# A down projection over a sliding range of input block pairs

## The chip, the cores and the metric

The kernel runs on one core of a Trainium2 chip. The metric is the device time of one execution in microseconds (us), the median of several runs. TensorE multiplies, VectorE (DVE), ScalarE (ACT) and GpSimd (POOL) work elementwise, and SyncE (SP) and ScalarE issue the DMAs that move data between HBM and the on-chip memory.

## The reference

The input is x, 1024 tokens by 1024 features in float32. Two layers follow, the first with a chunked bidirectional mLSTM as its mixer, the second with windowed attention, each followed by a dense feed-forward block; every block begins with an RMS norm and is added to x. The change touches the feed-forward blocks:

```python
D_FF = -(-(8 * D_MODEL) // (3 * 256)) * 256   # 2816

def swiglu(h, w_in, w_out):
    gu = h @ w_in
    gate, up = gu[..., :D_FF], gu[..., D_FF:]
    return (jax.nn.silu(gate) * up) @ w_out

for i in range(DEPTH):                        # DEPTH = 2
    hn = rmsnorm(x, norm_mix_w[i])
    x = x + ...                               # mLSTM (i = 0) or windowed attention (i = 1)
    x = x + swiglu(rmsnorm(x, norm_ffn_w[i]), ffn_w_in[i], ffn_w_out[i])
return rmsnorm(x, norm_final_w)
```

## The kernel before

**Arithmetic.** A float32 product is made of three passes over operands that are split into a high and a low part: high by high, high by low, low by high. Splitting takes ScalarE for the high part (a copy into the rounded type, L203) and VectorE for the low part (the difference, L204). All matmuls are 128x128 weights by 512 columns.

**Feed-forward block.** The 2816 hidden features are 22 blocks of 128, taken as 11 pairs (p, p + 11). The down projection (`ffn_down`, L683) makes its eight output row blocks in pairs (e, e + 4), e = 0..3. For each it runs a 2x2 Strassen-Winograd step (`strassen`, L567 on): seven products in place of eight, summed over the input pairs. One pair costs 7 products by 3 passes = 21 matmuls. The products come in the order a11 b11, s4 b22, a12 b21, s2 t2, s1 t1, s3 t3, a22 t4, where a and s are blocks and sums of the weights, b and t blocks and sums of the hidden rows.

**Chunks and steps.** The 11 pairs are three chunks, `CHUNKS = ((0, 4), (4, 8), (8, 11))`; for each chunk e runs over 0..3, so FFN 0 has 12 steps: eight over four pairs, four over three. In FFN 1 the last chunk goes through `down_plain` (L742, matmuls on L759) in token halves, with no Strassen step. Each step reads two row blocks of x from memory (`xkeep`, L711), adds its products (L714 to L726) and writes them back (L730).

**Forms.** The hidden rows b and t are kept in HBM (`hkeep`), four tiles for each pair: the up projection writes them. `hidden_forms` (L545) loads those of the next chunk (hraw) during the last step of a chunk and splits them: for each pair one split of 512 columns (f) and three of 1024 (fh, fl). They then serve four steps. `left` (L507) makes the weight forms of the next step: wah/wal (needed by the first product), wch/wcl (s3, s4), wbh/wbl (s1, s2) and wd, from sums s12 and s34. Forms, weights, x and raw loads are units of a shared pool (46 units of 128 x 1032 floats); the four pairs of a chunk hold 28.

**Norm behind FFN 0.** In the last four steps each finished row block is scaled and split for the next product (`norm_split_row`: hnh on L207, hnl on L208) and its square is added to R (`norm_square_row`: L299 on ScalarE, L300 on VectorE). `norm_sums` (L372) then sums R over partitions by TensorE, and `spread` (L384 to L391) turns the result into a row factor. The attention's first product (L231) follows; its weights are cut into wh (L190, ScalarE) and wl (L191, GpSimd).

**Order.** Each engine takes its instructions in a fixed order. The program is written as above with small callbacks between the products (`more` for a part of the next weights, `rolled` for a group of forms, `taken` for adds to x); the tile framework sets the order on each engine when the program is built, from the order in which it is written, the dependencies of tiles, and when a pool has a free unit. An instruction that waits holds all behind it on its engine.

Of the kernel before, what the change touches and what calls it, by code (L numbers as in the profile page):

```python
# [11 lines left out]
F32 = mybir.dt.float32  # L12
# [24 lines left out]
CHUNKS = ((0, 4), (4, 8), (8, 11))  # L37
# [7 lines left out]
def _pieces(n, bits):  # L45
    rest = Fraction("6.28318530717958647692528676655900576839433879875021164194988918461563281257")
    out = []
    for _ in range(n):
        step = Fraction(2) ** (math.floor(math.log2(float(rest))) - bits + 1)
        q = (rest / step).__floor__() * step  # L50
        out.append(float(q))
        rest -= q
    return out

# [28 lines left out]
class Trunk:  # L83
# [32 lines left out]

    def slab(self, dtype=F32, name="slab"):
        return Pair([self.unit(dtype, name) for _ in range(2)])
# [24 lines left out]
    def sources(self):  # L143
        h = self.h
        cols = lambda src: [src[:, o:o + D] for o in range(0, src.shape[-1], D)]
        out = [h["m_gate"]]
        for u in range(3 * NH):
            out += cols(h["m_in"][u])
        for u in range(4):
            out += cols(h["m_out"][u])  # L150
        ffn = [[], []]
        for i in range(2):
            for p in range(NP):
                for f in (p, p + NP):
                    ffn[i] += cols(h["ffn_in"][i, f])
            for p0, p1 in CHUNKS:
                ffn[i] += [h["ffn_out"][i, d, :, 2 * p0 * P:2 * p1 * P] for d in D_ORDER]
# [170 lines left out]
    def norm_forms(self, i):  # L328
# [10 lines left out]
        f12 = pair("f12")  # L339
        ya = self.unit(name="ya")  # L340
        A.activation(ya, xa, AF.Copy, scale=wa)
        t12, t34 = self.unit(name="t12"), self.unit(name="t34")
# [153 lines left out]
    def left(self, m=HALF):  # L496
# [3 lines left out]
        a11, a12, a21, a22 = g[:, lo_], g[:, hi_], u[:, lo_], u[:, hi_]  # L500
        wide = (lambda: self.t([P, S], F32, "s", self.spare)) if self.spare else (lambda: self.unit(name="s"))
        s12, s34 = wide(), wide()
        pair = lambda n: tuple(self.unit(F32R, n + x)[:, :2 * m] for x in "hl")
        two = lambda f, c: (f[0][:, c], f[1][:, c])
        out = {}

        def one():  # L507
            wa = pair("wa")
            self.split(*wa, g)
            out["a11"], out["a12"] = two(wa, lo_), two(wa, hi_)  # L510
            V.tensor_tensor(s12[:, lo_], a21, a22, op=ALU.add)
            V.tensor_tensor(s12[:, hi_], s12[:, lo_], a11, op=ALU.subtract)

        def two_():
            V.tensor_tensor(s34[:, lo_], a11, a21, op=ALU.subtract)
            V.tensor_tensor(s34[:, hi_], a12, s12[:, hi_], op=ALU.subtract)
            wc = pair("wc")
            self.split(*wc, s34[:, :2 * m])
            out["s3"], out["s4"] = two(wc, lo_), two(wc, hi_)

        def three_():
            wb = pair("wb")
            self.split(*wb, s12[:, :2 * m])
            out["s1"], out["s2"] = two(wb, lo_), two(wb, hi_)

        def four():
            wd = self.unit(F32R, "wd")
            out["a22"] = (wd[:, :m], wd[:, m:2 * m])
            self.split(*out["a22"], a22)
# [15 lines left out]
    def hidden_forms(self, i, p0, p1):  # L545
        lo_, hi_ = slice(0, HALF), slice(HALF, S)
        forms = [{} for _ in range(p0, p1)]
# [6 lines left out]
        def single(p):  # L554
            raw = load(p, 0, lo_)
            f = self.unit(F32R, "f1")
            forms[p - p0]["b11"] = f[:, lo_], f[:, hi_]
            self.split(f[:, lo_], f[:, hi_], raw)

        def double(p, j, a, b):  # L560
# [3 lines left out]
            forms[p - p0][a] = f[0][:, lo_], f[1][:, lo_]  # L564
            forms[p - p0][b] = f[0][:, hi_], f[1][:, hi_]

        def group(f, *args):  # L567
            return lambda: [f(p, *args) for p in range(p0, p1)]

        return forms, [group(single), group(double, 1, "b21", "b22"), group(double, 2, "t1", "t2"), group(double, 3, "t3", "t4")]  # L570


    def hidden_plain(self, i, p0, p1):
# [8 lines left out]
        todo = [(p, j) for j in range(2) for p in range(p0, p1)]  # L582
# [42 lines left out]
    def ffn_up(self, i, side=()):  # L625
# [5 lines left out]
        plain = CHUNKS[-1][0] if i else NP  # L631
        forms = self.forms
        for n in range(NF):
            p, second = n // 2, n % 2
            roll = ()
            if n + 1 < NF:
                nxt, todo = self.left()
            else:
                nxt, todo = self.left((CHUNKS[0][1] - CHUNKS[0][0]) * P)
                self.dforms, roll = self.hidden_forms(i, *CHUNKS[0])  # L640
            more = lambda: todo.pop(0)() if todo else None
            hs = self.unit(name="hs")
# [28 lines left out]
            elif p < plain:  # L671
                t12, t34 = self.unit(name="t12"), self.unit(name="t34")
# [3 lines left out]
                V.tensor_tensor(t34[:, lo_], hs[:, hi_], ha[:, hi_], op=ALU.subtract)  # L676
                V.tensor_tensor(t34[:, hi_], hs[:, lo_], t12[:, hi_], op=ALU.subtract)
                nc.scalar.dma_start(self.hkeep[i][p][3], t34)
# [5 lines left out]
    def ffn_down(self, i, which, final=False):  # L684
# [3 lines left out]
        cur, forms = self.cur, self.dforms  # L688
        for ci, (p0, p1) in enumerate(CHUNKS):
            last = ci == len(CHUNKS) - 1  # L690
            if last:
                self.norm_begin(which, "final" if final else "plain")
                if final:
                    self.down_plain(p0, p1)
                    return
                self.x = [None] * KT
            for e in range(4):
                nxt, todo, roll = None, [], ()
                if e < 3:
                    nxt, todo = self.left((p1 - p0) * P)  # L700
                elif not last:
                    q0, q1 = CHUNKS[ci + 1]
                    if final and ci + 2 == len(CHUNKS):
                        roll = self.hidden_plain(i, q0, q1)
                    else:
                        nxt, todo = self.left((q1 - q0) * P)
                        nforms, roll = self.hidden_forms(i, q0, q1)
                more = lambda: todo.pop(0)() if todo else None
                xa, xb = self.unit(name="x"), self.unit(name="x")
                for x, d in ((xa, e), (xb, e + 4)):  # L710
                    nc.sync.dma_start(x, self.xkeep[d])  # L711

                def one(st):
                    V.tensor_tensor(xa[:, lo_], xa[:, lo_], st["a"], op=ALU.add)  # L714
                    V.tensor_tensor(xa[:, hi_], xa[:, hi_], st["c"], op=ALU.add)
                    V.tensor_tensor(xa[:, hi_], xa[:, hi_], st["e"], op=ALU.add)  # L716
                    G.tensor_tensor(xa[:, hi_], xa[:, hi_], st["u2"], op=ALU.add)  # L717

                def two(st):
                    V.tensor_tensor(xb[:, hi_], xb[:, hi_], st["c"], op=ALU.add)  # L720
                    G.tensor_tensor(xb[:, hi_], xb[:, hi_], st["u3"], op=ALU.add)

                def three_(st):
                    u3 = st["u3"]
                    V.tensor_tensor(u3, st["d"], u3, op=ALU.add)
                    V.tensor_tensor(xb[:, lo_], xb[:, lo_], u3, op=ALU.add)  # L726

                self.strassen(cur, forms, more, roll, (one, two, three_))
                for x, d in ((xa, e), (xb, e + 4)):
                    nc.scalar.dma_start(self.xkeep[d], x)  # L730
                    if last:
                        self.x[d] = x
                        self.norm_split_row(d)
                        self.norm_square_row(d)
                cur = nxt
            if not last:
                forms = nforms if nxt else None
        self.norm_end()

    def down_plain(self, p0, p1):  # L740
        nc = self.nc
        hs = [self.hs[p, j] for j in range(2) for p in range(p0, p1)]  # L742
# [468 lines left out]
    def rope_tables(self):  # L1211
# [3 lines left out]
        ang, kh, r1, kl = (self.t([P, Q], F32, f"tab{i}", 1) for i in range(4))  # L1215
# [307 lines left out]
    def run(self):  # L1523
        self.setup()
        self.mlstm()
        with self.phase("f0", 9, dict(mm=6, mx=2), 2):
            self.attn_setup()
            self.ffn_up(0, self.rope_tables())
# [27 lines left out]
def arrange(inp):  # L1556
# [19 lines left out]
    for hh in range(NH):  # L1576
# [21 lines left out]
    order = [f + o for p0, p1 in CHUNKS for o in (0, NP) for f in range(p0, p1)]  # L1598
    out["ffn_out"] = np.ascontiguousarray(
        fo.reshape(2, NF, P, KT, P)[:, order].transpose(0, 3, 2, 1, 4)  # L1600
    ).reshape(2, KT, P, NF * P)
# [20 lines left out]
```

## Time and profile before

| | |
|---|---|
| median of 3 runs | 2376.28 us (2373.6 to 2376.89) |
| profiled execution, its own time | 2373.66 us |
| its span | 2371.7 us |
| TensorE busy | 2199.7 us, 93% |
| weight loads busy (beside the matmuls) | 1789.9 us, 75% |
| VectorE busy | 1645.4 us, 69% |
| ScalarE busy | 902.7 us, 38% |
| GpSimd busy | 554.1 us, 23% |
| mean granted TensorE clock | 0.967 |

The span is the stretch from the first to the last instruction that the profile shows; about 2 us of the execution lie around it. FFN 0's down projection runs from 964 to 1206 us, FFN 1's from 2099 to the end. Times in rows are counted from the span's start.

### The profile page before, as it was taken

The page shows a single profiled execution, that of the slowest core. Times are in us where ns is not written, and L with a number is a line of the kernel's source. Part 1 is how long each engine was busy: PE and PEld are TensorE (multiplying, and loading weights), DVE is VectorE, ACT ScalarE, POOL GpSimd, SP SyncE. Part 2 cuts the span into 40 slices and gives each one's busy share as a digit, 9 for nine tenths or more (in the row PEclk, how much of TensorE's full clock was granted, in tenths as well). Part 3 has the DMA queues.
Part 4 walks back from the last instruction along what each step waited for, and adds up shares of the span by engine and source line. Part 5 has one row for each costly group of instructions (what it writes and reads, how often), then busy time and mean ns, then how long its engine had stood idle before and what let it go on. Part 6 is the DMA issues. An engine that isn't in the chain of part 4 may idle for free. (4 is left out here: it accounts for less than half of the span.)

```text
span 2371.7 us, 28532 instructions
## 1 busy us (share of the span) xinstructions
PE 2199.7 (93%) x10379; PEld 1789.9 (75%) x10379; DVE 1645.4 (69%) x2954; ACT 902.7 (38%) x1616; POOL 554.1 (23%) x398
## 2 busy tenths in 40 slices
PE   6999998989999999899979888799899999999988
PEld 3889888867888888677758666587788888867767
DVE  5455666698777777777863666787877777677723
ACT  3334445343222222432422666774422222242322
POOL 4312213301111111111123444560111111111133
PEclk9999999999999999999979899999999999999999
DMA  3111114133232323675624233702223232266552
GB/s 118 51 36 45 63 36 151 50 108 107 95 120 98 116 98 132 231 260 180 226 102 146 67 114 104 239 17 98 89 98 126 88 133 98 82 212 247 182 191 72
DMA packets 95788, 286.12 MB, mean 121 GB/s; under 512 B 10736, under 2 KB 17776, under 8 KB 95648
## 3 DMA queue, kind: packets, MB, share of 16 engines
q1 hardware_dynamic: 73960, 209.71, 27.0%
q10 hardware_dynamic: 21688, 74.59, 7.9%
q8 instruction: 82, 1.34, 0.2%
q14 instruction: 58, 0.48, 0.1%
HBM read 191.53 MB, written 92.73 MB: 120 GB/s over the span
## 5 line engine op out<-in xcount | busy, mean ns | idle before, releaser
L191 POOL TENSOR_TENSOR wl<-raw,wh 128x1024 fp32r<-128x1024 f32 (+2 forms) x56 | 128.6, 2301 | 352.9 <-ACT wh L190 283.5
L651 POOL TENSOR_TENSOR t<-t,R 128x512 f32<-128x512 f32 x44 | 63.9, 1452 | 613.3 <-ACT t L650 613.3
L231 PE MATMUL mm<-slab,wh 128*128 128x512 f32 x512 | 153.5, 409 | 11.1 <-ACT wh L190 8.3
L539 PE MATMUL mm<-f,wah 128*128 128x512 f32 x504 | 159.3, 397 | 3.2 <-DVE x L793 2.4
L539 PE MATMUL mm<-f12h,wbh 128*128 128x512 f32 x352 | 138.8, 395 | 0.4 <-ACT wbh L203 0.4
L539 PE MATMUL mm<-f12l,wbh 128*128 128x512 f32 x352 | 138.8, 394 | 0.0
L539 PE MATMUL mm<-f12h,wbl 128*128 128x512 f32 x352 | 138.5, 394 | 0.0
L607 DVE TENSOR_TENSOR t<-mm,t 128x512 f32<-128x512 f32 x64 | 44.2, 691 | 128.0 <-PE mm L539 128.0
L231 PE MATMUL mm<-hnh,wh 128*128 128x512 f32 x416 | 127.8, 409 | 1.6 <-ACT wh L190 1.6
L650 ACT ACTIVATE t<-t 128x512 f32<-128x512 f32 x44 | 27.9, 634 | 256.3 <-DVE t L649 256.3
L231 PE MATMUL mm<-hnl,wh 128*128 128x512 f32 x416 | 125.2, 402 | 0.0
L231 PE MATMUL mm<-hnh,wl 128*128 128x512 f32 x416 | 124.6, 399 | 0.0
L231 PEld LDWEIGHTS mm<-slab,wh 128*128 128x128 f32 x512 | 96.3, 194 | 33.6 <-ACT wh L190 10.1
L596 ACT ACTIVATE t<-mm 128x512 f32<-128x512 f32 x64 | 38.4, 600 | 215.2 <-PE mm L539 197.6
L539 PE MATMUL mm<-f34h,wd 128*128 128x512 f32 x352 | 117.2, 394 | 0.0
L1404 POOL TENSOR_TENSOR e<-e,smd 128x768 f32<-128x768 f32 (+1 forms) x64 | 87.4, 1368 | 123.2 <-DVE smd L1403 78.2
L539 PEld LDWEIGHTS mm<-f,wah 128*128 128x128 f32 x504 | 95.1, 189 | 26.4 <-ACT wah L203 4.5
L1392 DVE CUSTOM_DVE_ANT_0 e<-sc,mask,nsink 128x384 f32<-128x384 f32 (+1 forms) x128 | 72.8, 577 | 46.2 <-PE sc L1387 44.9
L539 PE MATMUL mm<-f,wal 128*128 128x512 f32 x252 | 100.7, 400 | 4.2 <-DVE wal L204 4.2
L717 POOL TENSOR_TENSOR x<-x,t 128x512 f32<-128x512 f32 x20 | 30.2, 1512 | 308.4 <-DVE x L716 163.4
L1387 PE MATMUL sc<-slab,slab 128*128 128x384 f32 (+1 forms) x256 | 68.1, 348 | 33.9 <-DMA slab<-bounce 21.2
L203 ACT ACTIVATE wah<-raw 128x1024 fp32r<-128x1024 f32 (+1 forms) x64 | 66.5, 1039 | 74.5 <-DMA hkeep<-hs 33.2
(330 smaller groups left out, 6381.8 us busy)
## 6 DMA issues: line engine op xcount, KB each, us to landing
raw<-in_ffn_in_dram SPq DMA_DIRECT2D x88, 512.0 KB
hraw<-hkeep SPq DMA_DIRECT2D x63, 512.0 KB
xkeep<-x ACTq DMA_DIRECT2D x56, 512.0 KB
hkeep<-hs ACTq DMA_DIRECT2D x44, 512.0 KB
x<-xkeep SPq DMA_DIRECT2D x40, 512.0 KB
hkeep<-t ACTq DMA_DIRECT2D x38, 512.0 KB
raw<-in_ffn_out_dram SPq DMA_DIRECT2D x32, 512.0 KB
raw<-in_m_in_dram SPq DMA_DIRECT2D x24, 512.0 KB
```

The source lines that it names most:

```text
L191: (nc.vector if fast else nc.gpsimd).tensor_tensor(lo[:, c], r[:, c], hi[:, c].bitcast(F32), op=ALU.subtract)
L203: self.nc.scalar.activation(hi, src, AF.Copy)
L231: self.nc.tensor.matmul(st["ps"], lhsT=l, rhs=r, start=j == 0, stop=j == len(jobs) - 1)
L539: self.nc.tensor.matmul(ps, lhsT=l[a][:, c], rhs=r[b], start=start and k + a + b == 0, stop=stop and k == last and a == 1, skip_group_chec ...
L596: A.activation(p1, pa, AF.Copy)
L607: V.tensor_tensor(u2, pb, p1, op=ALU.add)
L650: A.activation(g0, g0, AF.Silu)
L651: G.tensor_tensor(g0, g0, R0, op=ALU.mult)
L717: G.tensor_tensor(xa[:, hi_], xa[:, hi_], st["u2"], op=ALU.add)
L1387: T.matmul(ps[:, :n], lhsT=lq, rhs=kk[:, j * S + k0 * P:j * S + (k0 + nk) * P], start=j == 0, stop=j == 1,)
L1392: V.tensor_tensor_reduce(out=e[:, hd, :n], in0=ps[:, :n], in1=self.mask[:, m0:m0 + n], scale=1.0, scalar=self.nsink[:, s], op0=ALU.add, op ...
L1404: G.tensor_tensor(e[:, j:j + 2, :n], e[:, j:j + 2, :n], d.unsqueeze(2).broadcast_to([P, 2, n]), op=ALU.mult,)
```

## The change

The chunks go. A table gives for each step its output pair and its input pairs; the range of pairs slides, and a step loads and splits only the pairs that the step before did not hold. FFN 0 still has 12 steps (the first over three pairs, eight over four, three over three), FFN 1 eight steps over four pairs and then the same plain tail. Pair 0 is loaded and split a second time in FFN 0, pairs 0 and 1 in FFN 1. The matmul count stays 10297; SyncE issues 537 DMAs in place of 525. The down weights lie in HBM in the order of the steps.

```diff
-CHUNKS = ((0, 4), (4, 8), (8, 11))
+STEPS = (
+    ((0, (0, 1, 2)), (1, (0, 1, 2, 3)), (2, (0, 1, 2, 3)), (3, (1, 2, 3, 4)),
...
+    ((0, (0, 1, 2, 3)), (1, (0, 1, 2, 3)), (2, (1, 2, 3, 4)), (3, (2, 3, 4, 5)),
...
+)
+PLAIN = (8, 9, 10)
...
-    def norm_square_row(self, d):
+    def norm_square_row(self, d, eng=None):
...
-            nc.vector.tensor_tensor(self.R, self.R, sq, op=ALU.add)
+            (eng or nc.vector).tensor_tensor(self.R, self.R, sq, op=ALU.add)
...
         def one():
-            wa = pair("wa")
+            s12, s34 = st["s"] = wide(), wide()
+            V.tensor_tensor(s12[:, lo_], a21, a22, op=ALU.add)
+            V.tensor_tensor(s12[:, hi_], s12[:, lo_], a11, op=ALU.subtract)
+            V.tensor_tensor(s34[:, lo_], a11, a21, op=ALU.subtract)
+            V.tensor_tensor(s34[:, hi_], a12, s12[:, hi_], op=ALU.subtract)
+            wa = unit("wah"), unit("wal")
             self.split(*wa, g)
...
-            elif p < plain:
-                t12, t34 = self.unit(name="t12"), self.unit(name="t34")
+            elif not i or p not in PLAIN:
+                t12 = self.wide("t12")
...
+                V.tensor_tensor(ha[:, hi_], hs[:, hi_], ha[:, hi_], op=ALU.subtract)
+                V.tensor_tensor(ha[:, lo_], hs[:, lo_], t12[:, hi_], op=ALU.subtract)
+                nc.scalar.dma_start(self.hkeep[i][p][3], ha)
...
+        steps = STEPS[i]
+        for n, (e, pairs) in enumerate(steps):
+            last = n + 4 >= len(steps) and not final
+            end = n + 1 == len(steps)
...
+            if not end:
+                after = steps[n + 1][1]
+                nxt, todo = self.left(len(after) * P)
+                new, roll = self.hidden_forms(i, [p for p in after if p not in pairs])
+            elif final:
+                new, roll = {}, self.hidden_plain(i, PLAIN)
...
+            E = V if end else G
+
+            def keep(x, d):
+                nc.scalar.dma_start(self.xkeep[d], x)
+                if last:
+                    self.x[d] = x
+                    self.norm_split_row(d)
+                    self.norm_square_row(d, E)
...
+                E.tensor_tensor(xa[:, hi_], xa[:, hi_], st["u2"], op=ALU.add)
+                keep(xa, e)
...
+                E.tensor_tensor(xb[:, hi_], xb[:, hi_], st["u3"], op=ALU.add)
...
                 V.tensor_tensor(u3, st["d"], u3, op=ALU.add)
                 V.tensor_tensor(xb[:, lo_], xb[:, lo_], u3, op=ALU.add)
+                if end and not final:
+                    self.ahead()
+                keep(xb, e + 4)
...
+            live = {p: f for p, f in live.items() if not end and p in after}
+            live.update(new if not end else {})
...
-        with self.phase("f0", 9, dict(mm=6, mx=2), 2):
+        with self.phase("f0", 9, dict(mm=6, mx=2), 3):
```

`ahead` cuts the next weight (wh, wl) before it is asked for. Of the square sums five go to GpSimd (the first of the eight is a copy, the last step's two stay on VectorE). The last argument of `phase` is the number of spare wide tiles for s, two before, three now; the rotary tables' four small tiles become one unit. Lines behind `strassen` shift by 18 to 21: L539 becomes L557, L204 L222, L372 L390, L231 L249; the adds to x are L735 to L738 (u2), L742, L743 (u3), L747 and L748.

The order on VectorE as FFN 0 enters its ninth step, before (a chunk seam; x_9518 and x_9519 are the row blocks of the eighth step, wal is the ninth's):

```order
L204 TENSOR_TENSOR wal_9566<-raw_9378,wah_9565 128x768
L714 TENSOR_TENSOR x_9518<-x_9518,mm_9522 128x512
L607 TENSOR_TENSOR t_1698_9614<-mm_9601,t_1678_9535 128x512
L204 TENSOR_TENSOR fl_9586<-hraw_9583,fh_9585 128x1024
L715 TENSOR_TENSOR x_9518<-x_9518,mm_9616 128x512
L720 TENSOR_TENSOR x_9519<-x_9519,mm_9616 128x512
L716 TENSOR_TENSOR x_9518<-x_9518,mm_9552 128x512
L616 TENSOR_TENSOR t_1711_9669<-mm_9601,t_1678_9535 128x512
L204 TENSOR_TENSOR fl_9592<-hraw_9589,fh_9591 128x1024
L725 TENSOR_TENSOR t_1711_9669<-mm_9677,t_1711_9669 128x512
L726 TENSOR_TENSOR x_9519<-x_9519,t_1711_9669 128x512
```

The weights' low part wal is made ahead of the eighth step's adds to x. Now, at the same place (x_9505 is the second row block of the eighth step, wal the ninth's weights, f and fl its new pairs):

```order
L742 TENSOR_TENSOR x_9505<-x_9505,mm_9595 128x512
L222 TENSOR_TENSOR f_1675_9525<-hraw_9523,f_1675_9525 128x512
L747 TENSOR_TENSOR t_1700_9641<-mm_9649,t_1700_9641 128x512
L748 TENSOR_TENSOR x_9505<-x_9505,t_1700_9641 128x512
L222 TENSOR_TENSOR f_1677_9530<-hraw_9528,f_1677_9530 128x512
L222 TENSOR_TENSOR wal_9553<-raw_9343,wah_9552 128x1024
L222 TENSOR_TENSOR fl_9571<-hraw_9568,fh_9570 128x1024
L222 TENSOR_TENSOR fl_9577<-hraw_9574,fh_9576 128x1024
L222 TENSOR_TENSOR fl_9611<-hraw_9608,fh_9610 128x1024
L222 TENSOR_TENSOR fl_9617<-hraw_9614,fh_9616 128x1024
L222 TENSOR_TENSOR wcl_9626<-s_9547,wch_9625 128x1024
```

What moved is wal: it stands behind L747 and L748, the last adds of the eighth step, which take that step's last product, and behind a split of the new pairs.

TensorE at the end of FFN 0, before (L539 is the last down product, L372 the sums of the norm, L389 and L390 the spread, L231 the attention's first product):

```order
L539 MATMUL mm_10170<-fl_9705,wd_10077 128x512
L539 MATMUL mm_10170<-fh_9704,wd_10077 128x512
L372 MATMUL mx_10253<-ones,R_9715 128x1 x4
L372 MATMUL mx_10268<-ones,R_9715 128x1 x4
L389 MATMUL mx_10318<-t_1839_10308,ones 128x512
L390 MATMUL mx_10318<-t_1840_10309,ones 128x512
L389 MATMUL mx_10332<-t_1842_10322,ones 128x512
L390 MATMUL mx_10332<-t_1843_10323,ones 128x512
L231 MATMUL mm_10222<-hnh_9829,wh_10218 128x512
L231 MATMUL mm_10222<-hnh_9954,wh_10218 128x512
```

Now, from the last down product on (L249 is the attention's first product):

```order
L557 MATMUL mm_10187<-fl_10089,wd_10102 128x512
L557 MATMUL mm_10187<-fh_10088,wd_10102 128x512
L249 MATMUL mm_10231<-hnh_9773,wh_10201 128x512
L249 MATMUL mm_10231<-hnh_9904,wh_10201 128x512
L249 MATMUL mm_10231<-hnh_10048,wh_10201 128x512
```

Nineteen rows further on, all of L249 (L390 are the sums of the norm, L249 into mm_10292 the second half):

```order
L249 MATMUL mm_10231<-hnh_10206,wh_10201 128x512
L249 MATMUL mm_10231<-hnl_10207,wh_10201 128x512
L249 MATMUL mm_10231<-hnh_10206,wl_10202 128x512
L390 MATMUL mx_10262<-ones,R_9680 128x1 x4
L249 MATMUL mm_10292<-hnh_9773,wh_10201 128x512
L249 MATMUL mm_10292<-hnh_9904,wh_10201 128x512
L390 MATMUL mx_10277<-ones,R_9680 128x1 x4
L249 MATMUL mm_10292<-hnh_10048,wh_10201 128x512
L249 MATMUL mm_10292<-hnh_10167,wh_10201 128x512
```

The product's first 24 matmuls moved ahead of the norm's sums, and the second half begins between them.

## Rows read from the trace of the kernel before

**Rows 1.** The page, part 1: busy time of each engine.

```profile
PE 2199.7 (93%) x10379; PEld 1789.9 (75%) x10379; DVE 1645.4 (69%) x2954; ACT 902.7 (38%) x1616; POOL 554.1 (23%) x398
```

**Rows 2.** Stretches: us, busy us and count of each engine, clock, DMA, GB/s.

```profile
964.45:995.33 30.88, 23.98 (x85) 16.93 (x83) 24.75 (x30) 15.07 (x18) 0.83 (x1) 0.89 0.54 173
995.33:1016.84 21.51, 20.15 (x84) 15.73 (x85) 20.30 (x26) 7.13 (x9) 6.22 (x4) 1.00 0.74 263
1036.28:1055.76 19.48, 19.48 (x86) 15.77 (x84) 10.02 (x14) 5.70 (x8) 3.27 (x2) 1.00 0.89 306
1055.76:1083.58 27.82, 23.45 (x85) 17.02 (x84) 22.16 (x24) 15.88 (x18) 0.05 (x1) 0.88 0.58 209
1142.00:1161.73 19.73, 17.26 (x64) 12.74 (x63) 15.70 (x19) 10.43 (x13) 0.40 (x1) 0.91 0.57 207
1161.73:1176.49 14.76, 14.76 (x65) 11.75 (x63) 14.76 (x21) 7.32 (x9) 3.26 (x2) 1.00 0.38 145
...
2098.83:2128.11 29.28, 23.76 (x85) 16.96 (x84) 22.51 (x26) 16.93 (x19) 0.83 (x1) 0.88 0.52 175
2186.96:2215.67 28.71, 23.81 (x85) 17.42 (x84) 20.81 (x23) 15.78 (x18) 0.06 (x1) 0.88 0.57 201
2278.72:2294.82 16.10, 11.53 (x39) 8.18 (x39) 1.85 (x3) 3.23 (x4) 5.71 (x4) 0.82 0.98 352
```

**Rows 3.** Timeline of TensorE at the seam of 1055.76: start, us, operation, wait.

```profile
1059.41 0.50 PE L539 MATMUL mm<-fh,wah 128*128 128x512 f32 x1 [0.69 <-ACT t L596]
...
1066.04 0.79 PE L539 MATMUL mm<-fh,wch 128*128 128x512 f32 x1 [2.55 <-ACT wch L203]
...
1068.43 0.79 PE L539 MATMUL mm<-fh,wcl 128*128 128x512 f32 x1 [0.65 <-DVE wcl L204]
...
1070.73 0.63 PE L539 MATMUL mm<-fl,wch 128*128 128x512 f32 x1
1071.16 0.63 PE L539 MATMUL mm<-fh,wcl 128*128 128x512 f32 x1
```

**Rows 4.** Stretches behind two seams, columns as in rows 2.

```profile
1065.54:1072.37 6.83, 5.68 (x12) 3.92 (x13) 6.80 (x9) 6.65 (x8) 0.00 (x0) 0.50 0.78 300
1150.87:1154.29 3.42, 3.42 (x10) 2.64 (x9) 3.35 (x6) 3.42 (x6) 0.00 (x0) 0.50 0.45 183
```

**Rows 5.** Stretch and timeline at the end of FFN 0, all engines.

```profile
1206.44:1242.33 35.89, 18.72 (x69) 14.88 (x69) 15.94 (x44) 7.29 (x8) 11.73 (x8) 0.67 0.19 66
...
1210.62 0.69 DVE L725 TENSOR_TENSOR t<-mm,t 128x512 f32<-128x512 f32 x1 [2.15 <-POOL x L721]
...
1217.29 1.84 PE L372 MATMUL mx<-ones,R 128*128 128x1 f32 x8 [10.85 <-DVE R L300]
...
1224.99 0.76 PE L389 MATMUL mx<-t,ones 128*128 128x512 f32 x1 [3.74 <-issue]
...
1229.72 3.29 PE L231 MATMUL mm<-hnh,wh 128*128 128x512 f32 x7 [1.63 <-ACT wh L190]
...
1242.33 0.86 PE L231 MATMUL mm<-hnh,wh 128*128 128x512 f32 x3
```

**Rows 6.** Costs by form: VectorE and GpSimd; rows of the square sums; ScalarE's cuts.

```profile
L204 DVE TENSOR_TENSOR fl<-hraw,fh 128x1024 fp32r<-128x1024 f32 x33 | 38.7, 1219 | 5.2 <-ACT fh L203 5.2
L204 DVE TENSOR_TENSOR wbl<-s,wbh 128x1024 fp32r<-128x1024 f32 x8 | 12.0, 1504 | 1.0 <-DMA xkeep<-x 1.0
...
L204 DVE TENSOR_TENSOR f<-hraw,f 128x512 fp32r<-128x512 f32 x7 | 4.7, 689 | 4.6 <-ACT f L203 4.6
...
L191 POOL TENSOR_TENSOR wl<-raw,wh 128x1024 fp32r<-128x1024 f32 x47 | 113.5, 2415 | 338.7 <-ACT wh L190 283.5 <-PE pk L215 38.0 <-issue 15.8
...
L300 DVE TENSOR_TENSOR R<-R,sq x21: 1211/1219/3435, 495.0 to 1674.4; 128x1024 f32<-128x1024 f32 x21
...
1209.77 1.15 ACT L207 ACTIVATE hnh<-x,nw 128x1024 fp32r<-128x1024 f32 x1 [6.91 <-POOL x L717]
...
1228.62 2.00 ACT L190 ACTIVATE wh<-raw 128x1024 fp32r<-128x1024 f32 x2
```

More of the change, by code (lines that the diff above doesn't have):

```diff
@@ L53, in _pieces, with down_order @@
     return out
+def down_order(i):
+    out = [(d, pairs) for e, pairs in STEPS[i] for d in (e, e + 4)]
+    return out + [(d, PLAIN) for d in D_ORDER] if i else out
 def weave(main, fill=()):
@@ L115, in unit, with wide @@
         return self.sl.tile([P, UNIT], dtype, name=self.nm(name), tag="unit")[:, :S]
+    def wide(self, tag):
+        return self.unit(name=tag)
     def slab(self, dtype=F32, name="slab"):
@@ L155, in sources @@
                     ffn[i] += cols(h["ffn_in"][i, f])
[L156 to L157 removed]
+            at = 0
+            for d, pairs in down_order(i):
+                ffn[i].append(h["ffn_out"][i, :, at:at + 2 * len(pairs) * P])
+                at += 2 * len(pairs) * P
         att = []
@@ L542, in seven, with hidden_forms @@
                 )
-    def hidden_forms(self, i, p0, p1):
+    def hidden_forms(self, i, pairs):
         lo_, hi_ = slice(0, HALF), slice(HALF, S)
-        forms = [{} for _ in range(p0, p1)]
+        forms = {p: {} for p in pairs}
         def load(p, j, cols):
@@ L580, in get @@
             self.split(*self.hs[p, j], raw)
-        todo = [(p, j) for j in range(2) for p in range(p0, p1)]
+        todo = [(p, j) for j in range(2) for p in pairs]
         n = -(-len(todo) // 4)
@@ L638, in ffn_up @@
             else:
-                nxt, todo = self.left((CHUNKS[0][1] - CHUNKS[0][0]) * P)
-                self.dforms, roll = self.hidden_forms(i, *CHUNKS[0])
+                pairs = STEPS[i][0][1]
+                nxt, todo = self.left(len(pairs) * P)
+                self.dforms, roll = self.hidden_forms(i, pairs)
             more = lambda: todo.pop(0)() if todo else None
-            hs = self.unit(name="hs")
+            hs = self.wide("hs")
             R0, R1 = self.Rv(0), self.Rv(1)
@@ L687, in ffn_down @@
         lo_, hi_ = slice(0, HALF), slice(HALF, S)
[L688 to L695, printed above, removed]
-                self.x = [None] * KT
[L697 to L737, printed above, removed]
@@ L741, in down_plain @@
+        if final:
+            self.norm_begin(which, "final")
+            self.down_plain(PLAIN)
+        else:
+            self.norm_end()
+    def down_plain(self, pairs):
         nc = self.nc
-        hs = [self.hs[p, j] for j in range(2) for p in range(p0, p1)]
+        hs = [self.hs[p, j] for j in range(2) for p in pairs]
         self.load_x(self.xkeep)
@@ L1214, in rope_tables @@
         Q = S // 4
-        ang, kh, r1, kl = (self.t([P, Q], F32, f"tab{i}", 1) for i in range(4))
+        tab = self.unit(name="tab")
+        ang, kh, r1, kl = (tab[:, i * Q:(i + 1) * Q] for i in range(4))
         def put(i, tab):
@@ L1597, in arrange @@
     ).reshape(2, NF, P, 2 * D)
[L1598 to L1601, printed above, removed]
+    fo = fo.reshape(2, NF, P, KT, P)
+    out["ffn_out"] = np.stack([
+        np.concatenate([fo[i, p + o, :, d] for d, pairs in down_order(i) for o in (0, NP) for p in pairs], axis=1)
+        for i in range(2)
+    ])
     return out
```

66 lines of the change are left out of this document (38 added, 28 removed), and 3 rows, old and new, of the table STEPS.

## Prediction

> **What bounds the kernel now.** I read the page's shares first, then the table of stretches cut at the starts of the down projection's steps, then TensorE's timeline at the seams, then the costs by form. TensorE is busy 93% of the span [rows 1]: nothing gets faster here unless TensorE waits less, for the change keeps its matmul count. A step over four input pairs is 84 matmuls. Undisturbed it takes 19.48 us, over three pairs 14.76 us [rows 2], which is 0.232 us a matmul and 4.87 us a pair. The steps that begin a chunk are longer: 30.88 us behind the up projection and 27.82 and 19.73 us at the two chunk seams of FFN 0, 29.28 and 28.71 us in FFN 1 [rows 2]. Over the undisturbed step these lose 11.4, 8.3, 5.0, 9.8 and 9.2 us; with 2.0 us in the second step (21.51) FFN 0 loses 26.7 us and FFN 1 19 us and a little.
>
> What a seam loses is seen in rows 3. TensorE waits 0.69 us for ScalarE's copy of the first product, 2.55 us for the high part of the next weights (wch, queued behind six fh splits) and 0.65 us for wcl (behind the fl splits on VectorE). Then its clock falls: from 1070.73 to 1071.16 one matmul takes 0.43 us instead of 0.23. The stretches at granted clock 0.50, the 1.2 GHz level, are 6.83 us behind waits of about 4 us and 3.42 us behind waits of 2.5 us [rows 4]; a matmul there costs 0.2 us more, so 3.2 and 1.6 us. The second step, 2.0 us late, kept clock 1.00 [rows 2]: short waits need not bring the clock down.
>
> The other loss is the end of FFN 0. From the last down matmul (1206.44) to the third half of the attention's first product (1242.33) pass 35.89 us, for 48 product matmuls and 12 of the norm. TensorE waits for the last square sums until 1217.29, for the spread of the row factor until 1224.99, and for the first cut weight until 1229.72; clock 0.67 [rows 5].
>
> **The change part by part.** All sums start at the profiled execution, 2373.66 us (2.6 below the median, inside the runs' 2373.6 to 2376.89).
>
> End of FFN 0. The 24 matmuls of the first half now stand ahead of the norm's sums, 22 of the second ahead of the spread. They need the cut weight: with u2 and u3 added on VectorE the two GpSimd adds, on which L725 waited 2.15 us [rows 5], leave the path, and the cut is issued in the last step. From rows 6, two trailing adds 1.4, hnh 1.15, two cuts (2.00 us together) and their handovers: the first product about 4.8 us behind the last down matmul. Then 48 matmuls at 0.232 (11.1), sums 3.7 (two groups at the times of rows 5), spread 0.8: 20.4; about half of it at the low clock, +3: 23.4 against 35.9. I take -12.5. Ends: -6 (all 48 at 0.43) and -15.5 (none).
>
> First step. Now over three pairs: 63 matmuls, 14.6 us, while VectorE's 24.75 us of work there [rows 2] stays: one pair's splits (0.69 and three of 1.22, 4.35 us, rows 6) go to the next step, which begins a pair's matmuls earlier. Ends: 0, when the same VectorE work takes the same time, and +4.9, a pair's matmuls no longer beside it. I take +3.5.
>
> Sliding steps. I call them s0 to s11. The intent is that VectorE's bursts are spread: a seam's 22.16 us of VectorE [rows 2] becomes 10 to 15 us a step plus 4.35 per new pair, under 19.5 everywhere. But the order on VectorE changes too. At the seam before, wal of the next step stands ahead of x's adds; now, where new pairs come in, it stands behind L747 and L748, and L747 waits for the step's very last product. So the third matmul of the next step waits for two adds, f and wal, three times 0.69 (the 512-column form) and 1.22 [rows 6], less the 0.46 us of two matmuls: 2.8 us. Behind it follow the old seam's waits, with two pairs' splits instead of four: 0.7 for the copy, then wch and wcl, 2.7 by adding durations along the queues. With an allowance of 0.5 us for GpSimd's u3 and the low clock (1.5, the shorter stretch of rows 4) this is about 8 us for s4 and s8 each, where before lost 8.3 and 5.0. The same order with one new pair stands ahead of s5 and s11 (wal 3.5 us late by the queue, clock +1.5 to +2: 5.5 and 5); s3 and s7 wait 1.3 each for the copy and wch; s9 and s10, over three pairs, where VectorE is busy all of 14.76 us already [rows 2], 1.9 each. Sum: 16+10.5+2.6+3.8=33 against 13.3 (8.3 and 5.0): +19.7. Ends: -8 (only 0.7 for the copy at seven steps) and +27 (every wait over 2 us brings the 6.83 us stretch).
>
> The sums of squares go to GpSimd in three of the last four steps: five adds. VectorE loses four of 1.22, GpSimd gains five of about 2.4 (its 1024-wide form, rows 6). VectorE's R add itself has a longest case of 3.435 against 1.219 [rows 6], and wbl a mean of 1.504: such operations run long where GpSimd adds at the same time. The Trainium skill ("SBUF — State Buffer", "Who interferes with whom") says that a VectorE instruction with two SBUF inputs and a GpSimd instruction that reads SBUF exclude each other, the later one waiting out the first. By that rule the move gives nothing back, five times 2.4 us of lockout for four of 1.22; the trace agrees as far as the 3.435 us case goes. In the sum: 0, ends -2 and +5, since the last three steps have 1.2 us adds on either side.
>
> FFN 1. The range slides at five places. The seam at 2186.96 (9.2) gives way to about 13.7 (0.6, 3.5, 6, 0.6, 2.5 and some clock, by the same queue sums): +4.5, ends -6 and +9. Its plain tail, 16.10 us at clock 0.82 with DMA 0.98 busy [rows 2], has the first cut weight behind five splits of the hidden rows: +1.5, ends 0 and +3. Up projections (t34 in place, one more spare): an allowance of +0.4, ends -1 and +2. Twelve loads of 512 KB come twice, 6 MB: DMA share in the steps is 0.5 to 0.9, no term.
>
> Sum: -12.5+3.5+19.7+0+4.5+1.5+0.4=+17.1, 2391 us.
>
> **The rivals.** First, the spreading does what it is for: waits for wal hide, since GpSimd and ScalarE are ahead in a step that is not a burst. Sliding steps then lose the 0.7 us copy and little else: FFN 0 -8, FFN 1 -6, end -12.5, first step +3.5, tail +1.5: -21.5, 2352; with half of the wal waits left (five of 2.8, half: 7, and the clock twice: 3) 2362. For it: VectorE's sum per step fits, 10.02 us in a step without splits [rows 2]. Against: wal's place in the queue is fixed, however fast the engines are.
>
> Second, the waits come but the clock stays, as in the second step before (2.0 us, clock 1.00): the slides lose 6.3 us less, FFN 1 2, the first step 3.2 and the end 3: 17.1-14.5=+2.6, 2376, no change to be seen.
>
> Third, slower than forecast: the units run out. 46 units carry 28 live forms, eight of weights, x and raw; with a sliding range new forms are taken while old ones are still read. If the load of the new pairs waits for a unit that the last product frees, each of eleven sliding steps gets a load's wait; the seam shows 2.55 us for a queue of splits [rows 3], so 11 x 2.5=27 in place of some 10 that the forecast already holds: 2408. It decides where the hidden rows' loads start only when TensorE enters the next step. "Perfetto Trace Analysis" of the Trainium skill ("Optimization Strategy") reads a gap that repeats regularly on the engine that should be full as too little SBUF for the next tile. Before there are no such gaps inside a chunk (19.48 us steps), so nothing shows it yet.
>
> **How the numbers follow.** Forecast (slower by 6 to 30 us) 0.56; first rival 0.24; second 0.10; third 0.10. A difference under 0.2%, 4.8 us, can't be told from none here: faster 0.24, within 0.10, slower 0.66. Range 2360 to 2408: below it lies the full form of the first rival, and the units' case ends it above; the forecast's own range is 2381 to 2403.
>
> **What would show it.** Right: starts of s4, s5, s8 and s11 have TensorE waiting 2 to 4 us on wal, released by VectorE, then again on wch or wcl, at clock 0.5; the stretch from the last down matmul of FFN 0 to the third half of the attention's product is 21 to 26 us; the first step loses 13 to 18 us with the second. Wrong: sliding steps of 19.5 to 20 us each, or an end of FFN 0 still over 30 us, for then products wait for the cut weight, not for the norm. Of GpSimd: VectorE operations of over 2 us beside 2.4 us adds of R.

## The result, and the profile after

The changed kernel takes 2429.84 us (median of 4 runs, 2424.74 to 2432.03) against 2374.94 for the kernel before: ratio 1.023, interval 1.0209 to 1.0252, 55 us slower. Slower was forecast, but by 17 us; the measured time lies 22 us above the range. The profiled execution took 2429.81 us, its span 2427.8.

The page, part 1:

```profile
span 2427.8 us, 28527 instructions
## 1 busy us (share of the span) xinstructions
PE 2219.8 (91%) x10379; PEld 1802.7 (74%) x10379; DVE 1666.2 (69%) x2965; ACT 907.7 (37%) x1627; POOL 559.5 (23%) x399
```
TensorE's busy time grew by 20 us for the same count of matmuls (2219.8 against 2199.7 [rows 1]), at a mean granted clock of 0.958 against 0.967. The other 36 us of the span are waits. The stretches that answer to [rows 2] (us; busy us and count of TensorE, weight loads, VectorE, ScalarE, GpSimd; clock; DMA share; GB/s) are s0, s1, s3, s4, s5, s8 to s11 of FFN 0, the end of FFN 0, and two steps of FFN 1:

```profile
962.32:988.10 25.78, 18.76 (x65) 13.08 (x63) 20.23 (x26) 10.81 (x13) 0.39 (x1) 0.86 0.53 190
988.10:1016.05 27.95, 22.35 (x84) 17.28 (x85) 21.29 (x26) 9.18 (x11) 4.89 (x4) 0.82 0.59 209
1035.54:1059.33 23.79, 19.88 (x85) 15.50 (x83) 15.89 (x20) 7.19 (x10) 3.06 (x3) 1.00 0.76 264
1059.33:1087.83 28.50, 24.72 (x84) 18.13 (x85) 17.00 (x21) 10.27 (x12) 0.00 (x0) 0.82 0.53 190
1087.83:1115.52 27.69, 21.29 (x86) 16.59 (x85) 21.46 (x27) 9.16 (x11) 4.87 (x4) 0.94 0.53 170
1156.60:1182.52 25.92, 20.82 (x86) 15.45 (x85) 17.08 (x21) 9.54 (x11) 0.47 (x1) 1.00 0.54 181
1182.52:1201.95 19.43, 15.67 (x65) 11.51 (x63) 15.11 (x19) 7.31 (x9) 4.93 (x3) 1.00 0.25 96
1201.95:1224.20 22.25, 17.71 (x65) 13.09 (x63) 17.82 (x21) 7.92 (x10) 8.52 (x5) 0.85 0.54 190
1224.20:1248.97 24.77, 17.23 (x64) 12.39 (x62) 17.35 (x17) 9.29 (x11) 8.24 (x4) 0.93 0.45 154
1248.97:1273.14 24.17, 16.93 (x70) 13.28 (x69) 16.16 (x42) 6.74 (x8) 4.57 (x3) 0.86 0.24 82
2206.50:2239.60 33.10, 24.03 (x85) 18.17 (x84) 21.09 (x26) 8.16 (x11) 5.89 (x4) 0.81 0.65 222
2239.60:2264.54 24.94, 22.87 (x84) 16.87 (x85) 15.43 (x17) 11.66 (x13) 0.00 (x0) 0.91 0.51 169
```
Over the undisturbed 19.48 and 14.76 us of before, s0 and s1 lose 11.0 and 8.5 us, s3 4.3, s4 9.0, s5 8.2, s8 6.4, s9 4.7, s10 7.5, s11 10.0 us. The stretch 2206.50 to 2239.60 of FFN 1 loses 13.6 us, more than any seam of before. The end of FFN 0 (the tenth row) takes 24.17 us where before took 35.89 [rows 5].

By stretches, after against before: up to FFN 0's down projection -2.1 us, FFN 0's down projection 286.65 against 241.99 (+44.7), its end -11.7, the attention behind that +7.4, FFN 1's up projection -0.9, all from FFN 1's down projection on 291.73 against 272.87 (+18.9). The sum is +56.3; the spans differ by 56.1.

What TensorE waited for most over FFN 0's down projection (us in total, times, longest), before:

```profile
PE mm L539 <- ACT wch L203: 6.1, 3, 2.5
...
PE mm L539 <- DVE wal L204: 0.8, 2, 0.5
```
and after:

```profile
PE mm L557 <- DVE wal L222: 18.2, 5, 5.7
PE mm L557 <- ACT t L614: 10.0, 10, 1.8
PE mm L557 <- ACT wch L221: 9.0, 6, 2.5
```
The wait for wal is the largest and grew most. How s5 begins, on five queues (start, us, engine, line, operation, and in brackets the idle time before it with its releaser; a q behind the engine's name marks the issue of a DMA):

```profile
1069.51 15.82 SPq L569 DMA_DIRECT2D hraw<-hkeep  x4
1088.02 3.48 SPq L189 DMA_DIRECT2D raw<-in_ffn_out_dram  x2
...
1089.32 1.27 POOL L738 TENSOR_TENSOR x<-x,t 128x512 f32<-128x512 f32 x1 [30.35 <-DVE x L737]
...
1090.54 1.72 POOL L743 TENSOR_TENSOR x<-x,t 128x512 f32<-128x512 f32 x1
1090.62 4.50 ACTq L728 DMA_DIRECT2D xkeep<-x  x2
...
1092.30 0.69 DVE L747 TENSOR_TENSOR t<-mm,t 128x512 f32<-128x512 f32 x1 [1.15 <-POOL x L743]
1092.90 1.22 DVE L222 TENSOR_TENSOR wal<-raw,wah 128x1024 fp32r<-128x1024 f32 x1
1094.04 0.68 DVE L748 TENSOR_TENSOR x<-x,t 128x512 f32<-128x512 f32 x1
...
1094.17 0.79 PE L557 MATMUL mm<-f,wal 128*128 128x512 f32 x1 [5.71 <-DVE wal L222]
...
1095.22 1.06 ACT L221 ACTIVATE fh<-hraw 128x1024 fp32r<-128x1024 f32 x1 [19.33 <-DMA raw<-in_ffn_out_dram]
```
Read it from TensorE back: it waits 5.71 us for wal, and wal's split stands on VectorE behind L747, which waits for the two GpSimd adds u2 and u3 one behind the other, 1.27 and 1.72 us. On SyncE 15.82 us pass between the first and the last issue of the four loads of a new pair, which wait for their units: in this stretch three waits, 10.2 us in all, are for earlier splits and one of 8.4 us is for a product. The next weights are asked for only behind them, at 1088.02. ScalarE stood idle for 19.33 us and then has fh, the copy and wch to do at once. This wait is not for a load still under way: the last of the four was issued at 1085.01, and by 1088 the DMA traffic was down to 8 GB/s. What stands on ScalarE's queue ahead of fh until 1095.12 is the two writes of x, the second of which needs the add L748 of 1094.04. What shows at s5 is thus a split that stands late in its queue, and wal late in VectorE's.

The end of FFN 0, as forecast, in the order product, sums, product:

```profile
1255.31 3.35 PE L249 MATMUL mm<-hnh,wh 128*128 128x512 f32 x7 [6.34 <-ACT wh L208]
...
1263.51 0.95 PE L390 MATMUL mx<-ones,R 128*128 128x1 f32 x8
...
1273.14 1.89 PE L249 MATMUL mm<-hnh,wh 128*128 128x512 f32 x7 [0.21 <-ACT wh L208]
```

### The profile page after: what moved, and what is told of

The parts are those of the page before. It is cut to its first block, busy times and chain, and to the rows that moved or that the text cites. A ratio compares the mean times of both kernels' runs of the same rounds, so it can differ in the third digit from the quotient of the medians.

```text
span 2427.8 us, 28527 instructions
## 1 busy us (share of the span) xinstructions
PE 2219.8 (91%) x10379; PEld 1802.7 (74%) x10379; DVE 1666.2 (69%) x2965; ACT 907.7 (37%) x1627; POOL 559.5 (23%) x399
## 5 line engine op out<-in xcount | busy, mean ns | idle before, releaser
L557 PE MATMUL mm<-f,wah 128*128 128x512 f32 x504 | 168.8, 417 | 15.6 <-ACT wah L221 15.6
L249 PE MATMUL mm<-slab,wh 128*128 128x512 f32 x512 | 153.7, 410 | 8.0 <-ACT wh L208 5.1
L557 PE MATMUL mm<-f12h,wbh 128*128 128x512 f32 x352 | 139.2, 395 | 0.0
L557 PE MATMUL mm<-f12h,wbl 128*128 128x512 f32 x352 | 138.7, 394 | 0.0
L557 PE MATMUL mm<-f12l,wbh 128*128 128x512 f32 x352 | 138.6, 394 | 0.0
L249 PE MATMUL mm<-hnh,wh 128*128 128x512 f32 x416 | 128.6, 411 | 6.6 <-ACT wh L208 6.6
L557 PE MATMUL mm<-f,wal 128*128 128x512 f32 x252 | 106.5, 422 | 28.6 <-DVE wal L222 28.5
L557 PEld LDWEIGHTS mm<-f,wah 128*128 128x128 f32 x504 | 100.7, 201 | 40.9 <-ACT wah L221 17.8
L249 PE MATMUL mm<-hnl,wh 128*128 128x512 f32 x416 | 126.2, 405 | 0.0
L249 PE MATMUL mm<-hnh,wl 128*128 128x512 f32 x416 | 124.9, 400 | 0.0
L249 PEld LDWEIGHTS mm<-slab,wh 128*128 128x128 f32 x512 | 96.8, 194 | 28.3 <-ACT wh L208 6.3
L557 PE MATMUL mm<-f34h,wd 128*128 128x512 f32 x352 | 117.2, 394 | 0.0
L221 ACT ACTIVATE fh<-hraw 128x1024 fp32r<-128x1024 f32 x66 | 67.0, 1050 | 123.5 <-DVE x L748 48.5
L222 DVE TENSOR_TENSOR fl<-hraw,fh 128x1024 fp32r<-128x1024 f32 x66 | 79.0, 1220 | 40.2 <-ACT fh L221 40.2
```

Of the source, the lines that this page charges most:

```text
L221: self.nc.scalar.activation(hi, src, AF.Copy)
L222: (eng or self.nc.vector).tensor_tensor(lo, src, hi.bitcast(F32), op=ALU.subtract)
L249: self.nc.tensor.matmul(st["ps"], lhsT=l, rhs=r, start=j == 0, stop=j == len(jobs) - 1)
L557: self.nc.tensor.matmul(ps, lhsT=l[a][:, c], rhs=r[b], start=start and k + a + b == 0, stop=stop and k == last and a == 1, skip_group_chec ...
```

## The experiments

Ratios are to the kernel before, run beside it on the same chip, with 95% intervals; times are medians. The theories at the start: A, loads of new pairs come late, since they wait for units, and the weights' loads stand behind them on SyncE; B, wal stands on VectorE behind adds that wait for GpSimd; C, ScalarE's queue is held by the early write of x. D came with the result of r1: GpSimd's adds of the square sums hold up VectorE in the three-pair steps.

**r1: the table alone undone.**

```diff
-STEPS = (((0, (0, 1, 2)), (1, (0, 1, 2, 3)), ...
+_C = lambda a, b: tuple((e, tuple(range(a, b))) for e in range(4))
+STEPS = (_C(0, 4) + _C(4, 8) + _C(8, 11), _C(0, 4) + _C(4, 8))
```

> The changed kernel with the table alone put back to chunks (pairs 0-3, 4-7, 8-10 in FFN 0, 0-3 and 4-7 in FFN 1); all other edits stay. If the sliding range is what costs (all three theories below say so), about 2365 us: the kernel before, 2375, less some 10 for the end of FFN 0 and for the up projection. If other edits (weight sums first, xkeep writes early, GpSimd's square sums) cost most, over 2400.

Measured: 2381.22 us, 1.0027 (1.0012 to 1.0042). The sliding range costs 49 of the 55 us. The rest of the change is no gain either, though the end of FFN 0 gained: something in it costs about as much.

**r2: all adds on VectorE.**

```diff
-            E = V if end else G
+            E = V
```

> The changed kernel with the adds of u2, u3 and of the square sums on VectorE in all steps. Theory B (wal waits on VectorE behind L747, which waits for two GpSimd adds): falls by 20 us or more, to about 2405. Theory A (loads of new pairs wait on SyncE for units that the last product frees, the weights' loads behind them): moves by less than 8 us. Theory C (ScalarE's queue held by the early xkeep write that waits for GpSimd's u2): falls by about 10.

Measured: 2407.38 us, 1.0133 (1.0116 to 1.015): 22 us less. Theory B holds for that part of the loss, though not all of it is B: the square sums moved too, and r6 puts some 8 us on them.

**r3: the writes of x behind the step.**

```diff
-                nc.scalar.dma_start(self.xkeep[d], x)          # in keep()
...
             self.strassen(cur, [live[p] for p in pairs], more, roll, (one, two, three_))
+            for x, d in ((xa, e), (xb, e + 4)):
+                nc.scalar.dma_start(self.xkeep[d], x)
```

> The changed kernel with both writes of x to xkeep issued behind the step, as before the change. Theory C: falls by 15 us or more, to under 2415. Theories A and B: within 4 us of 2430.

Measured: 2434.11 us, 1.0243 (1.0228 to 1.0259). Theory C falls for the early write. At s5 both writes stand where they stood, ahead of fh and behind the step's last add, so r3 doesn't say what the second write costs.

**r4: no loads of hidden rows.** One tile is loaded once and all forms are split from it.

```diff
-            raw = self.unit(name="hraw")[:, cols]
-            self.nc.sync.dma_start(raw, self.hkeep[i][p][j][:, cols])
-            return raw
+            if self.fix[0] != i:
+                self.fix = (i, self.unit(name="fix"))
+                self.nc.sync.dma_start(self.fix[1], self.hkeep[i][0][0])
+            return self.fix[1][:, cols]
```

> The changed kernel without the loads of the hidden rows: every form is split from one resident tile (so the hidden rows that enter the product are not the right ones); the splits themselves, their count and their units stay. Theory A: nearly all of the sliding steps' loss (some 53 us in FFN 0, 21 in FFN 1) goes, about 2360. Theory B and C: the splits still stand in the queues, loss falls by less than 20 us, 2410 to 2425.

Measured: 2331.89 us, 0.9818 (0.9804 to 0.9833): 98 us less than the changed kernel with every split still done, and 45 less than the kernel before, whose seams waited for loads too. That is far below even theory A's 2360. The splits as work don't cost; what costs is that they depend on loads.

**r5: chunk table and square sums on VectorE; r6: the changed kernel with the square sums on VectorE.**

```diff
-                    self.norm_square_row(d, E)
+                    self.norm_square_row(d)
```

> The chunk table of r1 and, besides, the square sums back on VectorE; the end of FFN 0 (writes early, norm work and first attention weight inside the last step) as changed. Theory D, that GpSimd's five 2.4 us adds lock VectorE in the three-pair steps (they lost 7.9 and 7.1 us in r1, nothing before): about 2367, faster than before by 0.3 to 0.5%. If these steps lose for another reason (early writes on ScalarE's queue): about 2380.

> The changed kernel with only the square sums back on VectorE, the adds of u2 and u3 stay on GpSimd. Theory D: 2417 to 2420, since r2, which moved both, gained 12 of its 22 us in the last three-pair steps. Otherwise 2428 to 2432, and the gain of r2 came from u2 and u3.

Measured: r5 2377.82 us, 1.0005 (0.9996 to 1.0014), 3 less than r1, not 14: theory D explains only a part. r6 2421.39 us, 1.0189 (1.0175 to 1.0203), 8 us less than the changed kernel. GpSimd's adds of R in the changed kernel (duration least, median, most, in ns) and what lay beside one of them on VectorE:

```profile
L318 POOL TENSOR_TENSOR R<-R,sq x5: 2414/2550/3225, 1193.0 to 1238.3; 128x1024 f32<-128x1024 f32 x5
...
1234.56 2.75 DVE L222 TENSOR_TENSOR wcl<-s,wch 128x768 fp32r<-128x768 f32 x1 [0.30 <-ACT wch L221]
```
A 768-column wcl took 2.75 us beside such an add that began at 1233.93 and took 2.55; in the kernel before the same form took 0.95 us on average. That is what the Trainium skill's rule says ("SBUF — State Buffer", "Who interferes with whom"): the later of the two waits the other out.

**r7: the loads issued by GpSimd.**

```diff
-            self.nc.sync.dma_start(raw, self.hkeep[i][p][j][:, cols])
+            self.nc.gpsimd.dma_start(raw, self.hkeep[i][p][j][:, cols])
```

> The changed kernel with the hidden rows' loads issued by GpSimd in place of SyncE. Theory A1 (the weights' loads stand behind the hidden rows' loads in SyncE's queue, which wait for units): wal comes ahead of the step's last adds again, under 2410. Theory A2 (the hidden rows' loads themselves start too late, because units come free with the last product): 2420 to 2435. Against both: u2 and u3 wait behind loads on GpSimd, over 2440.

Measured: 2491.15 us, 1.0478 (1.0462 to 1.0494). The time is that of the third case, but the trace shows the reverse of its reason: u2 and u3 (L738, L743) wait for VectorE's adds, and the loads stand behind them.

```profile
1073.03 1.29 POOL L738 TENSOR_TENSOR x<-x,t 128x512 f32<-128x512 f32 x1 [25.46 <-DVE x L737]
1074.29 1.70 POOL L743 TENSOR_TENSOR x<-x,t 128x512 f32<-128x512 f32 x1
1075.94 3.21 POOL L569 DMA_DIRECT2D hraw<-hkeep  x6
...
1079.88 1.06 ACT L221 ACTIVATE fh<-hraw 128x1024 fp32r<-128x1024 f32 x1 [20.60 <-DMA hraw<-hkeep]
```
Over FFN 0's down projection ScalarE's fh splits waited 133.0 us for loads, in 17 waits; in the changed kernel the trace names none of them. So in r7 the loads come later still, and it takes 61 us more. It says nothing between A1 and A2.

**r8: 43 units in the pool** (`N_UNITS = 43`).

> The changed kernel with 43 units in the pool instead of 46. If units are what the loads of new pairs wait for: at least 10 us more, 2440 or over. If only the order on SyncE and VectorE counts: within 4 us of 2430.

Measured: 2430.79 us, 1.0228 (1.0214 to 1.0242). Three units fewer cost nothing that shows (1 us), so the count of units is not the limit.

**r9: the loads issued, but not used.** As r4, with the load into a unit of the pool put back ahead of the `return`.

> As r4, every form is split from one resident tile (so the hidden rows in the product are not the right ones), but the loads of the hidden rows are issued on SyncE again, into units of the pool, and nothing reads them. Theory A3 (what costs is that splits wait for loads that land late, and with them everything behind on ScalarE and VectorE): 2330 to 2345, as r4. Theory A1 (the loads cost by holding up the weights and x behind them on SyncE, by their units or by the DMA engines' time): 2390 or more.

Measured: 2346.03 us, 0.9878 (0.9863 to 0.9892). The loads' own time on SyncE, in units and on the DMA engines is worth 14 us; the other 84 come of the splits' dependence on them. That is not waiting alone, for the order on VectorE is another too. In r9, as in r4, wal stands ahead of the last add to x of the step before, by 6 to 17 us in r9; at s5:

```profile
1054.13 1.22 DVE L222 TENSOR_TENSOR wal<-raw,wah 128x1024 fp32r<-128x1024 f32 x1
...
1065.20 0.69 DVE L751 TENSOR_TENSOR x<-x,t 128x512 f32<-128x512 f32 x1
```
In the changed kernel wal begins within 2 us of that add at s1, s4, s5 and s8. The direct waits are small there: ScalarE's f splits waited 7.0 us for hidden rows' loads over FFN 0's down projection.

**r10: the sliding range with all else mended** (E = V; the norm work of a step that is not the last behind it; wal split ahead of the weight sums). **r11, r12: the chunk table with the norm work early only in the last step**, square sums on VectorE; r12 also has the weight sums in the old order.

```diff
-                keep(xa, e)
+                if end:
+                    keep(xa, e)
...
             self.strassen(cur, [live[p] for p in pairs], more, roll, (one, two, three_))
+            if not end:
+                keep(xa, e)
+                keep(xb, e + 4)
```

> The sliding range with all else mended that the runs so far found: all adds and square sums on VectorE, norm work behind its step except in the last one, weight sums in the order of before. If the sliding range loses by itself: 2395 to 2405, still over 20 us above the kernel before. If the other edits and the adds on GpSimd made the loss: 2380 or less.

> Chunk table, square sums on VectorE, and the early write, norm work and first attention weight only in the last step of FFN 0; in the steps ahead of it they stand behind the step as before the change. If ScalarE's early norm work is what the second and third three-pair steps of r5 lost (7.8 and 2.9 us, wch late): 2366 to 2369, faster than before by 0.3 to 0.4%. If not: 2377 as r5.

> As r11, with the weight sums in the order of before (wal split first). If the sums ahead of wal made the chunk seams of r5 1 us longer each and the second step of the up projections 3 us: 2 to 6 us below r11, about 2363. Otherwise as r11.

Measured: r10 2400.32 us, 1.011 (1.0088 to 1.0131): the sliding range loses by itself, 35 us against r11 (which has u2 and u3 on GpSimd where r10 has them on VectorE). r11 2364.93 us, 0.9956 (0.9943 to 0.9969), r12 2365.21 us, 0.9955 (0.9942 to 0.9968): both faster than before, and the order of the weight sums makes no difference. What r5 lost in the second three-pair step is on ScalarE: norm work (hnh, the square) ahead of the next weights' wch. The last row is the whole step, with columns as in [rows 2]:

```profile
1167.56 1.15 ACT L220 ACTIVATE hnh<-x,nw 128x1024 fp32r<-128x1024 f32 x1 [2.28 <-POOL x L733]
...
1168.61 1.04 ACT L309 ACTIVATE R<-x 128x1024 f32<-128x1024 f32 x1
1169.56 0.83 ACT L216 ACTIVATE wch<-s 128x768 fp32r<-128x768 f32 x1
...
1161.49:1183.91 22.42, 18.33 (x64) 13.53 (x63) 17.45 (x25) 7.29 (x9) 2.53 (x2) 0.85 0.28 105
```
In r11 the same step is

```profile
1162.86:1178.98 16.12, 15.14 (x64) 11.63 (x63) 14.78 (x21) 7.42 (x9) 3.27 (x2) 1.00 0.37 137
```

**r13: a ring of their own for the loads**, the only edit to the changed kernel; the memory is the same.

```diff
-N_UNITS = 46
+N_UNITS = 42
...
+        self.hp = pool("hp", 4)
...
-            raw = self.unit(name="hraw")[:, cols]
+            raw = self.hp.tile([P, UNIT], F32, name=self.nm("hraw"), tag="hraw")[:, :S][:, cols]
```

> The changed kernel, with only this edit: the loaded hidden rows get a ring of four units of their own and the pool 42 in place of 46, so that a load waits for an earlier split and not for a unit that a TensorE product frees. Memory is the same. Theory A3a (loads land late because the unit that they are given is freed by one of the step's last products): the loss of the sliding steps falls by 25 us or more, under 2405. Theory A3b (they land late because of the DMA engines' time, or because they are asked for late in the program): 2420 or more.

Measured: 2360.44 us, 0.9949 (0.9929 to 0.9969): 69 us less than the changed kernel, faster than before. What SyncE waited for in front of the loads of hidden rows, over FFN 0's down projection (us in total, times, longest), in the changed kernel and in r13:

```profile
SPq L569 <- PE mm L557: 48.8, 14, 8.4
...
SPq L569 <- DMA xkeep<-x: 27.7, 5, 7.3
```
```profile
SPq L570 <- DVE fl L223: 64.7, 24, 9.2
SPq L570 <- DVE f L223: 30.0, 8, 6.8
```
In the changed kernel these loads wait most for TensorE's products and for writes of x that free a unit; in r13 for earlier splits, all but 1 us. Steps s0, s4, s5 and s7 of r13, where the changed kernel took 25.78, 28.50, 27.69 and 21.60 us:

```profile
962.06:978.63 16.57, 15.32 (x64) 11.58 (x62) 14.04 (x21) 6.84 (x10) 1.55 (x1) 1.00 0.55 181
1046.27:1068.00 21.73, 19.71 (x86) 15.70 (x85) 15.89 (x21) 8.49 (x10) 3.90 (x2) 1.00 0.74 261
1068.00:1087.46 19.46, 19.46 (x85) 15.76 (x84) 17.06 (x25) 5.81 (x7) 5.11 (x3) 1.00 0.67 229
1109.47:1133.77 24.30, 21.04 (x86) 16.69 (x85) 18.66 (x23) 9.61 (x12) 4.05 (x3) 0.93 0.80 261
```
s7 is longer than it was, and s1, which isn't shown, still takes 27.74 us. In r13's build wal also stands ahead of the step's last adds again, as in r4 and r9. So the ring acts in two ways, by earlier loads and by the order that follows from them; these two were not separated in any run.

**r14, r15: r13 mended as r10 (u2 and u3 left on GpSimd); r15 asks for all new forms behind the first product. r16: r11 with the ring.**

```diff
         A.activation(p1, pa, AF.Copy)
-        rolled()
+        for _ in range(4):
+            rolled()
```

> The sliding range with the ring of r13, square sums on VectorE, norm work ahead of time only in the last step, weight sums in the old order; u2 and u3 on GpSimd. Under A3a the sliding range may now do what it was made for: 2350 to 2370, level with the chunk table of r11 (2365) or better. Under A3b: 2390 to 2400 as r10.

> As r14, and all four groups of new forms are asked for behind the step's first product in place of one group behind each of four products. If what is left of lateness is the place in the program: another 5 to 15 us below r14. If the forms' units or the engines bound it: as r14 or slower, since the splits of a step then stand in one burst.

> The control: r11 (chunk table) with the same ring of four and 42 units. Under A3a the seams of the chunks gain too, but only partly, since all of a chunk's forms are freed by the last step's products: 2355 to 2366. If the ring costs the pool units that it needs: over 2368.

Measured: r14 2356.92 us, 0.9926 (0.9908 to 0.9944); r15 2363.64 us, 0.9959 (0.9941 to 0.9976), no gain from asking earlier; r16 2347.4 us, 0.9887 (0.9864 to 0.991), the fastest of all. r16 lies below its forecast too. With early loads the chunk table is faster than the sliding range by some 9 us (r14 against r16), and without them by 35 to 49 (r10 against r11, the changed kernel against r1): in no pair of runs here does the sliding itself gain anything.

## Why the prediction was wrong in size

The direction was right, and two terms held in number. The end of FFN 0 gave -11.7 us for a forecast -12.5, by the order that was foreseen: the first product came 6.3 us behind the last down matmul for 4.8, and the rest took 17.8 us for 18.6. (In that sum about half of 48 matmuls at 0.2 us more each make 4.8 us, not 3.) The first two steps lost 19.5 us for 17, in part by luck: s1's 8.5 us are waits of 3.12 us for wah and 4.91 for wal, and the prediction had no wait for weights in s1.

The step that failed is the sum of the sliding steps, "+19.7", and with it FFN 1's "+4.5". Behind s1 the forecast had 33 us of loss and the trace shows some 52; FFN 0's down projection with its first step was put at +23.2 and came out at +44.7, FFN 1's at +6 and came out at +18.9. It was sized from durations added along the queues, as if every load had landed when its split came up. That did not hold in before either: ScalarE's f splits waited 25.0 us for loads, in three waits, and the ring gained the chunk table 17.5 us (r11 to r16). But there it touched two seams, and sliding made it wrong in seven steps of FFN 0. r4 and r9 show the splits' dependence on the loads to be worth 84 us, as waiting and as order on the engines together, and r13 what made it: a load was given a unit that one of the current step's last products frees. How much of the 84 is the one and how much the other stays open.

Of FFN 1's +18.9 the eight steps up to the tail's first product make +21.8 (201.7 us against 179.9). In that is the tail's wait for its first cut weight, 7.49 us against 3.94, for which the forecast had +1.5. From that product on the tail is 3.0 us shorter.

That is the mechanism of the third rival, which got a chance of 0.10, but the price there was wrong, and its point of decision too: it decides where loads wait for a product, not where the units are too few (r8, as far as three units tell). The bound that I took, 2.55 us a step from one seam, is far below the 15.82 us over which SyncE issued four loads ahead of s5, 8.4 of them a wait for one product.

wal behind L747 was seen rightly: TensorE waited for it 1.76, 5.71, 3.08 and 2.71 us in s4, s5, s8 and s11. But the allowance of 0.5 us for GpSimd was too small: L747 waits for u2 and u3 in a row, 3 us. r2 took 22 us off by moving all these adds, of which r6 puts 8 on the square sums and so, if the two add up, about 14 on u2 and u3.

The square sums were put at 0. They cost 8 us (r6). That three-pair steps s9 and s10 would lose 1.9 each was too little (4.7 and 7.5): the norm work and the writes of x early in these steps (r5 against r11, with the chunk table: 13 us) were not in the sum at all.

The first rival, that the spreading hides the waits, fails as the change was made. With a ring the time is the one that it gives (r13, r14: 2360 and 2357 for 2352 to 2362), but not for its reason, since the chunk table, which does not spread, gets to 2347 with the same ring (r16). The second, that the clock stays, fails: s1 and s4 ran at 0.82. The +7.4 us in the attention behind FFN 0, whose code is unchanged, took back most of the gain at the end; its cause was not tested.

## What to carry to other kernels

When a change makes loads run beside products in every step, ask what frees the buffer that each load is given. If it is the end of the product, the load comes late, and what is made from it, with all that stands behind, can move back in the engines' orders, whatever their busy shares say. A small ring that only the loads use, emptied by the split that follows, cost no memory here and took off 69 us, more than the 55 that were lost. With the chunk table it gained 17.5 us (r11 to r16); on the kernel before, as it stands, it was not run. Before work is moved to an idle engine or earlier in a step, look at what waits behind it in that queue, and at the operations that run longer beside it.

## What was not expected

- The same 46 units, divided as 42 and 4, changed the time by 69 us; 43 units in one pool instead of 46 changed it by 1.
- GpSimd's 1024-column add took 2.41 to 3.23 us in the three-pair steps, and beside one of them a VectorE operation of 0.95 us took 2.75.
- Loads issued on GpSimd's queue stood behind its adds to x and came later than on SyncE: 61 us more (r7).
- r16's runs spread from 2336.8 to 2355.54 us, more than the 2369 to 2380 of before beside them.
